# RWKV layer: the projection stage and the start stage get two pools each, the first group's loads move, the last three projections run in quarters

## The chip, the cores and the metric

The kernel runs on one core of one Trainium2 chip. The metric is device time in microseconds, the median of the runs. The engines are TensorE (PE), VectorE (DVE), ScalarE (ACT), GpSimd (POOL) and SyncE (SP, which only issues DMAs here). Each engine, and each engine's DMA queue, runs its instructions in its own order.

## The reference, cut to what matters

The program computes two blocks. The change is in the second one's even layer, an RWKV layer with 12 heads of 64 channels over 256 context and 512 latent tokens:

```python
def proj(h, shift_fn):
    u = h @ w_in
    s, gate_r, four, gate_f = jnp.split(u, [...], axis=-1)
    s = s + (shift_fn(s) - s) * mu                  # r, k0, v, wl, al are neighbour-mixed
    r, k0, v, (wl_f, wl_b), (al_f, al_b) = ...
    return ..., gate_r, four, gate_f

def rwkv_dir_terms(...):                             # for each of two directions
    decay = exp(-exp(-softplus(-(w0 + tanh(wl) @ w2)) - 0.5))
    a = sigmoid(a0 + al @ a2)
    kk = k0 * k_k;  kk = kk / norm(kk per head)
    k = k0 * (1 + (a - 1) * k_a)
    bonus = sum(r * k * r_k per head) * v
    return r, decay, k, v, kk, kk * a, bonus

def step(s, inp):                                    # over the tokens, forward and backward
    sa = einsum('bhij,bhj->bhi', s, kk_t)
    s = s * w_t - sa * b_t + v_t * k_t
    return s, einsum('bhij,bhj->bhi', s, r_t)

def finish(o, gate_r, four, gate_f):
    yr = group_norm(o) * silu(gate_r)
    yf = fourier_mix(four) * silu(gate_f)
    return concatenate([yr, yf]) @ w_out
```

## The kernel before

The even layer has three stages. In the **projection stage** (`even_project`) the input stands channel by channel in on-chip memory, as a high and a low float32r half (`hT`, `cT`). There are 30 projections of 128 output channels; each has eight steps, and a step six matmuls (three products for 512 latent and for 256 context tokens). The weights come through a ring (`weights`: load by SyncE, high half by ScalarE, low half by VectorE). A loop over six pairs of heads j runs, for each direction, low-rank matmuls (`rwkv_lora`), the scaled keys and decays on VectorE (`rwkv_prepare`, tiles `pkr`, `pbk`), and a small triangular product on TensorE (`rwkv_triangle`, tile `sa`), whose diagonal blocks GpSimd inverts later (`rwkv_invert`). Between them stand the projections of pair j + 1 in the order of `ahead_of`: `k0`, `r`, `key`, `v`, where `key` is `rwkv_kk`: a square on ScalarE, head sums on TensorE, a square root, a transpose that spreads it, a product. Then comes the pair's `bonus`, which ends with the tile `po` and its store, and a gate projection for the first four pairs. All results go to DRAM (`sp_kr`, `sp_bk`, `sp_wc`, `sp_v`, `sp_off`, `sp_dia`, `sp_inv`, `sp_o`, `sp_gr`, `sp_four`, `sp_gf`). Left over are projections 24 and 25 (gates of pairs 4 and 5), 26 and 27 (`four`), 28 and 29 (`gf`), and the two triangles of pair 5. Five of these eight pieces (24, triangle, 25, triangle, 26) run while the pool `even_p` is open.

In the **start stage** `rwkv_open` opens the right-hand pool with all tiles of the recurrence; its memory overlaps that of the closed `even_p`, and `reuse_waits="tile"` makes each tile wait for those it overlaps. `rwkv_start` then loads the first chunk group of pairs 0 and 1 (`load`, `load_b`, `load_k`: `wc`, `v`, `bk`, `kr`, ten loads), clears halves of `kr` and `xf`, loads the inverses (`rwkv_inverse`, 14 loads a pair: `xf`, `xt`, `off`), merges the 32-blocks of the inverses to 64 (`rwkv_merges`: `first`, `second`, each for two directions) and makes `values`, `scores`, `keys`. The last three projections (27, 28, 29) stand among them.

In the **chain stage** (`rwkv`) the recurrence runs chunk by chunk (`rwkv_chains`) for two pairs at a time in nine units; each unit's list `fill` of other work (the next group's loads, values, scores and keys) is spread over its slots. TensorE's order there is as written. Before it starts, the pools of `hT`, the weight ring and the first PSUM are closed, and the second group's tiles lie over them.

A scheduler orders the instructions of each engine by their place in the program and by when it expects them to be ready; `high_priority(offset=n)` moves an instruction n places forward, `manual_schedule` keeps TensorE's order as written.

Of the kernel before, what the change touches and what calls it, by code (L numbers as in the profile page):

```python
# [18 lines left out]
P = 128  # L19
# [7 lines left out]
NC = 12  # L27
# [6 lines left out]
HEAD = 0  # L34
HERE = 5
# [18 lines left out]
class Kern:  # L54
# [776 lines left out]
    def even_project(self, pool, hT, cT, sp):  # L831
# [3 lines left out]
        pt = lambda tag, shape, bufs=1, dt=F32: pool.tile(shape, dt, tag=tag, name=self.nm(tag), bufs=bufs)  # L835
# [45 lines left out]
        def gate(pool, n, dst):  # L881

            a, b = dense(n)
            s = pool.tile([P, 768], F32, tag="pg", name=self.nm("pg"), bufs=2)
# [6 lines left out]
        def plain(n, dst, func, pool):  # L891
            a, b = dense(n)
            s = pool.tile([P, 768], F32, tag="pg", name=self.nm("pg"), bufs=2 if pool is self.kp else 1)
# [25 lines left out]
        for j in range(6):  # L919
            q, x = ahead_of(j + 1) if j < 5 else [], terms[j]  # L920
            nc.scalar.dma_start(sp["v"][j], x["v"])
            if j == 5:
                for n in range(26 - LATE, 26 - LATE + EARLY):
                    ahead[n] = self.weights(ins["ev_w_in_2"][n], 1024)
            kds, late = [], []
            for d, (ls, ta) in enumerate(self.rwkv_lora(pt, j, wl, al)):
                kd, *tri = self.rwkv_prepare(pt, j, d, ls, ta, x["r"], x["k0"], x["kk"], sp)
                kds.append(kd)
                late.append(partial(triangles, j, d, *tri))
                if q:  # L930
                    q.pop(0)()
                    late.pop(0)()
            for p in q:
                p()
            self.bonus(pt, j, x["r"], x["v"], kds, sp)
            if j < 6 - LATE:
                gate(pool, 20 + j, sp["gr"][j])

        return ([p for j, f in zip(range(6 - LATE, 6), late)
                 for p in (partial(plain, 20 + j, sp["gr"][j], AF.Silu), partial(lambda f, pool: f(), f))]  # L940
                + [partial(plain, 26 + n, sp["four"][n], AF.Copy) for n in range(2)]
                + [partial(plain, 28 + n, sp["gf"][n], AF.Silu) for n in range(2)])

# [43 lines left out]
    def rwkv_open(self, last):  # L987

        R = self.r = {}
        pool = last.enter_context(self.tc.tile_pool(name="rwkv_l", bufs=1, side="right", reuse_waits="tile"))  # L990
        quads, wide, row = [P, NC, 32], [P, 2, 8, 2, 64], [P, 768]
        for n, shape, ks in (("s0", [P, 2, P], range(4)), ("w", [P, P], range(4)), ("rmask", [P, 256], (0,)),
                             ("sc", [P, 2, 8, P], (0, 2)), ("zs", [P, 8, 2, 64], (0, 2)),
                             ("kr", wide, (0, 2)), ("xf", [P, 2, NC, 64], range(2)), ("bw", [P, 8, P], range(2)),
                             ("wc", [P, 2 * NC], range(4)), ("v", row, range(2)), ("bk", wide, range(2))):
            self.some(pool, n, shape, ks)
        for n in ("xt", "off", "mt"):
            R[n] = pool.tile([P, 4, NC, 32], F32, name=n)
        self.c2["rmask"] = R["rmask"][0]
        self.nc.sync.dma_start(self.c2["rmask"], self.ins["c_rmask"])  # L1000
        self.units, self.sums, self.decay = {}, {}, {}
# [4 lines left out]
    def clear(self, t):  # L1006

        nc = self.nc
        nc.vector.memset(t[64:128, 0], 0.0)
        nc.scalar.activation(t[0:64, 1].rearrange("p i a t -> p i (a t)"), self.ident[0:64, None, :].to_broadcast([64, 8, P]),  # L1010
                             AF.Copy, scale=0.0)

    def clear_xf(self, i):
        for d in range(2):
            for q in (0, 64):
                r = slice(q + 32 * (1 - d), q + 32 * (1 - d) + 32)
                self.nc.scalar.activation(self.r["xf"][i][r, d, :, 32 * d:32 * d + 32],
                                          self.ident[r, None, 0:32].to_broadcast([32, NC, 32]), AF.Copy, scale=0.0)

    def rwkv_start(self, sp, rest):  # L1020

        R = self.r
# [7 lines left out]
        (*inv, load, _), (load_b, load_k, scaled, *work) = zip(*(self.rwkv_begin(j, sp) for j in range(2))), zip(*(self.rwkv_group(j, 0, sp) for j in range(2)))  # L1030
        first = list(zip(load, load_b, load_k, zip(*inv), scaled))
        for l, (v, b, k, i, w) in enumerate(first):
            v()
            b()
            k()
            self.clear(R["kr"][2 * l])
            w()
        for l, (v, b, k, i, w) in enumerate(first):
            for p in i:
# [6 lines left out]
    def rwkv(self, sp, out, mid, last):  # L1046
# [32 lines left out]
        for p in loads(1):  # L1079
            p()  # L1080
# [141 lines left out]
    def rwkv_group(self, j, t, sp):  # L1222
# [9 lines left out]
        kr, bk, sc, zs = R["kr"][i], R["bk"][j % 2][:, (j // 2 + t) % 2], R["sc"][i], R["zs"][i]  # L1232
# [16 lines left out]
        def load_k():  # L1249
            for h in range(2):  # L1250
                nc.sync.dma_start(rows(kr[H[h], h]).rearrange("p (d c) x -> p d (c x)", d=2), sp["kr"][j, H[h], sl])
            self.units[j][t] = kr, sc, zs

        def values():
            v, ps = self.units[j]["v"], self.bank()
# [9 lines left out]
        def keys(k):  # L1265

            ps = self.bank()
# [5 lines left out]
        def scores(d):  # L1273

            pp = [self.bank(), self.bank()]
# [242 lines left out]
    def even_layer(self, hT, dr, held, sp):  # L1518
        tc, nc, ins = self.tc, self.nc, self.ins
        mid, last = ExitStack(), ExitStack()  # L1520
        with (tc.tile_pool(name="subst", bufs=1, reuse_waits="tile") as fp,
# [9 lines left out]
            with tc.tile_pool(name="even_p", bufs=1, reuse_waits="tile") as pool:  # L1531
                self.log_gamma(pool)
                rest = self.even_project(pool, hT, cT, sp)
                for p in rest[:HERE]:
                    p(pool)
            self.rwkv_open(last)
            with tc.tile_pool(name="even_q", bufs=1, reuse_waits="tile") as pool:
                self.rwkv_start(sp, [partial(p, pool) for p in rest[HERE:]])
            self.third = None
        for n in ("h", "w", "ps"):  # L1540
            held[n].close()
        with tc.tile_pool(name="ps_rw", bufs=1, space=PSUM) as self.ps:
            w, rows = self.rwkv(sp, dr["mixed"], mid, last)
# [466 lines left out]
```

## Time and profile before

| | |
|---|---|
| median of 3 runs | 2719.97 us (2709.35 to 2733.05) |
| profiled execution, its own time | 2715.68 us |
| its span | 2713.9 us |
| TensorE busy, mean granted clock | 2543.7 us (94%), 0.976 |
| VectorE, ScalarE, GpSimd busy | 1766.9, 1051.9, 659.5 us |
| projection stage | from about 1640 us |
| first matmul of the chains | 2021.39 us |

All times of rows are microseconds from the start of the profiled execution's span. An idle time in brackets is the engine's wait just before the instruction, with the one that ended it. Line numbers are those of the kernel before.

### The profile page before, as it was taken

How to read it: one execution, taken by the hardware profiler on the slowest of the kernel's cores; microseconds unless marked ns; L12 is line 12 of the kernel's file. 1: busy time of each engine (PE TensorE's matmuls, PEld its weight loads, DVE VectorE, ACT ScalarE, POOL GpSimd, SP SyncE). 2: the span in 40 equal slices, each digit the busy share in tenths (PEclk: the TensorE clock that was granted, in tenths of full speed). 3: DMA queues.
4: the chain of work that ended last, by engine and by line, in shares of the span. 5: the costliest groups of instructions: out<-in, count | busy, mean ns of one | idle time of the engine just before them, and what ended most of it. 6: DMA issues, size and time to landing. Idle time of an engine off the chain costs nothing. (4 is left out here: it accounts for less than half of the span.)

```text
span 2713.9 us, 42105 instructions
## 1 busy us (share of the span) xinstructions
PE 2543.7 (94%) x16408; PEld 2057.5 (76%) x16408; DVE 1766.9 (65%) x3239; ACT 1051.9 (39%) x1859; POOL 659.5 (24%) x735
## 2 busy tenths in 40 slices
PE   7899999999999999999999979999978999899988
PEld 6666788878888666788788868777767887788886
DVE  8878648985348788469975348788538665353263
ACT  3354433344213444424344235444433453332252
POOL 0200111111001101111111020787756342500032
PEclk9999999999999999999999989999979999999999
DMA  4221233543323121225534233456576544022111
GB/s 139 74 67 64 69 117 121 183 150 108 126 78 100 39 84 61 78 95 187 183 125 145 101 130 106 142 163 166 160 197 176 122 128 172 26 76 66 63 47 48
DMA packets 181159, 304.00 MB, mean 112 GB/s; under 512 B 90560, under 2 KB 100416, under 8 KB 180576
## 3 DMA queue, kind: packets, MB, share of 16 engines
q1 hardware_dynamic: 173856, 277.18, 33.0%
q0 software_dynamic: 4224, 15.73, 1.9%
q10 hardware_dynamic: 2880, 8.39, 0.8%
q8 instruction: 130, 2.13, 0.3%
q14 instruction: 69, 0.57, 0.1%
HBM read 255.95 MB, written 45.29 MB: 111 GB/s over the span
## 5 line engine op out<-in xcount | busy, mean ns | idle before, releaser
L108 DVE TENSOR_TENSOR wlo<-raw,whi 128x1024 fp32r<-128x1024 f32 (+1 forms) x335 | 426.5, 1274 | 396.7 <-ACT whi L107 394.4
L120 PE MATMUL psacc<-hT_hi,whi 128*128 128x512 f32 (+1 forms) x1528 | 586.4, 384 | 14.7 <-DVE u L628 7.1
L122 PE MATMUL psacc<-hT_hi,wlo 128*128 128x512 f32 (+1 forms) x1528 | 580.5, 380 | 4.2 <-DVE wlo L108 4.1
L121 PE MATMUL psacc<-hT_lo,whi 128*128 128x512 f32 (+1 forms) x1528 | 582.1, 381 | 2.0 <-POOL hT_lo L115 1.5
L107 ACT ACTIVATE whi<-raw 128x1024 fp32r<-128x1024 f32 (+1 forms) x335 | 323.6, 967 | 632.0 <-PE psacc L121 218.6
L120 PEld LDWEIGHTS psacc<-hT_hi,whi 128*128 128x128 f32 x1528 | 292.2, 191 | 72.4 <-issue 21.2
L122 PEld LDWEIGHTS psacc<-hT_hi,wlo 128*128 128x128 f32 x1528 | 291.7, 191 | 64.1 <-DVE wlo L108 6.8
L121 PEld LDWEIGHTS psacc<-hT_lo,whi 128*128 128x128 f32 x1528 | 292.3, 191 | 52.6 <-issue 8.5
L167 POOL TENSOR_TENSOR rr<-rr,mhalf 128x1 f32<-128x1 f32 (+1 forms) x52 | 49.8, 962 | 495.0 <-DVE rr L162 495.0
L637 POOL TENSOR_TENSOR gl<-silu,gh 128x512 fp32r<-128x512 f32 x44 | 66.0, 1500 | 406.9 <-ACT gh L636 406.9
L1300 POOL TENSOR_TENSOR fs_m<-fs_g,fs_x 112x31 f32<-112x31 f32 (+15 forms) x186 | 134.5, 723 | 40.5 <-DMA fs_g<-sp_dia 26.4
L1302 POOL TENSOR_TENSOR fs_x<-fs_x,fs_m 112x31 f32<-112x31 f32 (+15 forms) x186 | 133.5, 718 | 14.6
L683 DVE CUSTOM_DVE_ANT_0 psmm<-adaw,adac 128x512 f32<-128x512 f32 x192 | 132.3, 720 | 6.6 <-ACT adac L677 6.6
L156 PE MATMUL psacc<-whi,ohT_lo 128*128 128x512 f32 x256 | 100.2, 392 | 0.8 <-POOL ohT_lo L115 0.8
L154 PE MATMUL psacc<-whi,ohT_hi 128*128 128x512 f32 x256 | 100.5, 393 | 0.0
L155 PE MATMUL psacc<-wlo,ohT_hi 128*128 128x512 f32 x256 | 100.1, 391 | 0.0
L376 PE MATMUL psacc<-wlo,gh 128*128 128x512 f32 x246 | 96.8, 394 | 0.0
L377 PE MATMUL psacc<-whi,gl 128*128 128x512 f32 x246 | 96.8, 394 | 0.0
L375 PE MATMUL psacc<-whi,gh 128*128 128x512 f32 x246 | 96.8, 393 | 0.0
L342 POOL TENSOR_TENSOR m<-m,gate 128x512 f32<-128x512 f32 x16 | 20.6, 1286 | 303.6 <-DVE gate L341 303.6
L476 DVE SCALAR_TENSOR_TENSOR cvy<-cvu,lconst,cvy 128x512 f32<-128x512 f32 x120 | 89.3, 766 | 1.4
L516 PE MATMUL psmm<-kT,qq 64*128 64x256 f32 (+3 forms) x224 | 72.2, 549 | 15.8 <-DVE smx L591 13.6
(590 smaller groups left out, 5337.3 us busy)
## 6 DMA issues: line engine op xcount, KB each, us to landing
raw<-w_up SPq DMA_DIRECT2D x88, 512.0 KB, 3.3
raw<-w_fm SPq DMA_DIRECT2D x60, 512.0 KB, 3.3
adaw<-ada_w SPq DMA_DIRECT2D x96, 256.0 KB, 2.8
raw<-w_down SPq DMA_DIRECT2D x44, 512.0 KB, 3.3
raw<-ev_w_in SPq DMA_DIRECT2D x30, 512.0 KB, 4.0
raw<-od_w_tm SPq DMA_DIRECT2D x24, 512.0 KB, 3.3
sp_kr<-pkr SPq DMA_DIRECT2D x12, 768.0 KB, 3.5
bk<-sp_bk SPq DMA_DIRECT2D x18, 512.0 KB, 6.3
```

Source lines behind the costliest of these rows:

```text
L107: nc.scalar.activation(hi[:, :n], raw[:, :n], AF.Copy)
L108: (eng or nc.vector).tensor_tensor(lo[:, :n], raw[:, :n], hi[:, :n].bitcast(F32), ALU.subtract)
L120: mm(out, whi, xhi, start=start, stop=False)
L121: mm(out, whi, xlo, start=False, stop=False)
L122: mm(out, wlo, xhi, start=False, stop=stop)
L154: mm(o[:, :ncol], xhi[:, k, sl], wh, start=k == 0, stop=False)
L155: mm(o[:, :ncol], xhi[:, k, sl], wl, start=False, stop=False)
L156: mm(o[:, :ncol], xlo[:, k, sl], wh, start=False, stop=k == nk - 1)
L375: mm(acc, xh[k][:, ts], w[0][:, s], start=k == 0, stop=False)
L683: nc.vector.tensor_tensor_reduce(d, w, c[:, j, :], 1.0, 0.0, ALU.mult, ALU.add, part[:, half, n, j:j + 1])
L1300: nc.gpsimd.tensor_tensor(mv, g[:, :t, t:t + 1].to_broadcast([112, t, w]), x[:, t:t + 1, t:].to_broadcast([112, t, w]), ALU.mult)
L1302: nc.gpsimd.tensor_tensor(x[:, :t, t:], x[:, :t, t:], mv, ALU.subtract)
```

## The change

The projection stage's pool is split in two: `even_l` (outer) holds `pkr`, `pbk`, `sa`, `pg`; `even_p` (inner) holds the rest and closes earlier. The recurrence's pool is split too: `rwkv_l` holds what the first loads fill and what the merges read, and is opened as soon as `even_p` closes; `rwkv_m` holds the rest and is opened after the triangles. The order at the end of the projection stage becomes: projection 24, bonus 5, loads of the first group and of the inverses (`rwkv_load`), projection 25, triangle, projection 26, triangle. In `ahead_of`, `v` goes ahead of `key`. The clears all run on VectorE. The last three projections are cut into quarters of two steps and stand with the merges, values, scores and keys in one written order for TensorE; the stores of 28 and 29 are issued by SyncE in `rwkv`, behind the second group's loads. Cut to its core (left out: the constants `HEAD` and `HERE`, the lines that only pass arguments on, `clear_xf`, which gets memsets like `clear`, and `slot` in `rwkv_group`):

```diff
-        pt = lambda tag, shape, bufs=1, dt=F32: pool.tile(shape, dt, tag=tag, ...)
+        pt = lambda tag, shape, bufs=1, dt=F32: (later if tag in ("pkr", "pbk", "sa") else pool).tile(
+            shape, dt, tag=tag, name=self.nm(tag), bufs=bufs)
...
+        def in_parts(n, dst, func, buf):
+            st = {}
+            def part(i):
+                if not i:
+                    st["w"] = self.weights(ins["ev_w_in_2"][n], 1024)
+                    st["ps"] = self.acc(), self.psum("av", 1) if n % 2 else self.acc()
+                (hi, lo), (a, b) = st["w"], st["ps"]
+                for k in (2 * i, 2 * i + 1):
+                    ks = slice(k * P, (k + 1) * P)
+                    for o, (xhi, xlo) in ((a, hT), (b[:, :256], cT)):
+                        self.mm3(o, hi[:, ks], lo[:, ks], xhi[:, k], xlo[:, k], k == 0, k == KT - 1)
+                if i == 3:
+                    s = buf()
+                    with self.tc.high_priority(offset=DRAIN):
+                        nc.scalar.activation(s[:, lat], a, func)
+                        nc.scalar.activation(s[:, ctx], b[:, :256], func)
+                    st["out"] = s
+            return [partial(part, i) for i in range(4)], lambda: (nc.scalar if n == 27 else nc.sync).dma_start(dst, st["out"])
...
-            return [partial(project, j, "k0", 6), partial(project, j, "r", 0), partial(key, j), partial(project, j, "v", 12)]
+            return [partial(project, j, "k0", 6), partial(project, j, "r", 0), partial(project, j, "v", 12), partial(key, j)]
...
-            self.bonus(pt, j, x["r"], x["v"], kds, sp)
+            if j < 5:
+                self.bonus(pt, j, x["r"], x["v"], kds, sp)
...
+        return (partial(plain, 24, sp["gr"][4], AF.Silu), lambda: self.bonus(pt, 5, x["r"], x["v"], kds, sp),
+                [partial(plain, 25, sp["gr"][5], AF.Silu), late[0], partial(plain, 26, sp["four"][0], AF.Copy), late[1]],
+                lambda bufs: [in_parts(n, dst, f, b) for (n, dst, f), b in
+                              zip(((27, sp["four"][1], AF.Copy), (28, sp["gf"][0], AF.Silu), (29, sp["gf"][1], AF.Silu)), bufs)])
...
     def clear(self, t):
-        nc.vector.memset(t[64:128, 0], 0.0)
-        nc.scalar.activation(t[0:64, 1].rearrange(...), self.ident[0:64, None, :].to_broadcast([64, 8, P]), AF.Copy, scale=0.0)
+        for h in range(2):
+            nc.vector.memset(t[64 - 64 * h:128 - 64 * h, h], 0.0)
...
+        begun, groups = ([f(j) for j in range(2)] for f in (lambda j: self.rwkv_begin(j, sp), lambda j: self.rwkv_group(j, 0, sp)))
+        for (*_, load, _), (load_b, load_k, *_) in zip(begun, groups):
+            load()
+            load_b()
+            load_k()
+        for inv0, inv1, *_ in begun:
+            inv0()
+            inv1()
+        self.first = [g[2:] for g in groups]
+
+    def rwkv_start(self, sp, rest):
+        for l, (w, *_) in enumerate(self.first):
+            self.clear_xf(l)
             w()
+            self.clear(self.r["kr"][2 * l])
+        a, b = (q[1:] for q in self.first)
+        first, second = ([p for j in range(2) for p in self.rwkv_merges(j)[i:i + 2]] for i in (0, 2))
+        (store, *stores), (x, y, z) = [r[1] for r in rest], [r[0] for r in rest]
+        with self.tc.manual_schedule(engines={mybir.EngineType.PE}):
+            for p in (x[:1] + first[:2] + x[1:2] + first[2:] + x[2:3] + second[:2] + x[3:] + [store] + second[2:] + a[:2] + y[:1] + a[2:4]
+                      + y[1:2] + a[4:] + y[2:3] + b[:2] + y[3:] + b[2:4] + z[:1] + b[4:] + z[1:]):
                 p()
-            self.clear_xf(l)
-        work = [q[0] for q in work] + mixed(self.rwkv_merges(0) + self.rwkv_merges(1), [q[1] for q in work])
-        for p in rest[:HEAD] + mixed(rest[HEAD:], work):
-            p()
+        return stores
...
-        for p in loads(1):
+        for p in loads(1) + stores:
             p()
...
-            with tc.tile_pool(name="even_p", bufs=1, reuse_waits="tile") as pool:
-                self.log_gamma(pool)
-                rest = self.even_project(pool, hT, cT, sp)
-                for p in rest[:HERE]:
-                    p(pool)
-            self.rwkv_open(last)
+            with tc.tile_pool(name="even_l", bufs=1, reuse_waits="tile") as later:
+                with tc.tile_pool(name="even_p", bufs=1, reuse_waits="tile") as pool:
+                    self.log_gamma(pool)
+                    gate, bonus, rest, tiles = self.even_project(pool, later, hT, cT, sp)
+                    gate()
+                    bonus()
+                self.rwkv_open(last)
+                self.rwkv_load(sp)
+                for p in rest:
+                    p()
+            self.rwkv_more(last)
             with tc.tile_pool(name="even_q", bufs=1, reuse_waits="tile") as pool:
-                self.rwkv_start(sp, [partial(p, pool) for p in rest[HERE:]])
-            self.third = None
+                self.third = None
+                own = lambda: pool.tile([P, 768], F32, tag="pg", name=self.nm("pg"), bufs=1)
+                other = lambda: hp.tile([P, 1024], F32, tag="raw", name=self.nm("raw"), bufs=1)[:, :768]
+                stores = self.rwkv_start(sp, tiles((own, other, own)))
```

## Rows read from the trace of the kernel before

**Rows 1.** Stretches: us, engines' busy time (instructions), TensorE clock, DMA share, GB/s.

```profile
1920.00:1940.00 20.00, 13.88 (x74) 10.79 (x72) 19.96 (x16) 8.73 (x14) 18.82 (x16) 1.00 0.59 186
1940.00:1960.00 20.00, 19.35 (x179) 17.08 (x180) 7.54 (x7) 8.03 (x15) 17.89 (x28) 0.91 0.54 151
...
2000.00:2020.00 20.00, 14.70 (x320) 13.15 (x318) 6.50 (x14) 8.11 (x16) 17.27 (x33) 0.57 0.69 179
2020.00:2040.00 20.00, 16.00 (x292) 13.86 (x286) 13.00 (x33) 7.08 (x22) 8.79 (x17) 0.75 0.69 177
```

**Rows 2.** TensorE's timeline, 1926 to 2030: start, us, instruction [idle before, released by].

```profile
1929.43 1.53 PE L1442 MATMUL psmm<-bsum,c_blk 128*128 128x512 f32 x4 [3.48 <-DVE bsum L1439]
...
1940.65 2.29 PE L1196 MATMUL psmm<-pkr,pbk 64*64 64x64 f32 x48 [3.28 <-DVE po L1443]
...
2004.77 2.07 PE L1278 MATMUL pstr<-kr,bk 64*128 64x128 f32 x8 [4.32 <-ACT mt L1338]
...
2021.39 0.69 PE L1386 MATMUL psch<-zs,kr 64*64 64x64 f32 x7 [1.17 <-ACT xf L1349]
...
2028.88 1.38 PE L1278 MATMUL psms<-kr,bk 64*128 64x128 f32 x10
```

**Rows 3.** SyncE's queue in order of time, 1940 to 2010.

```profile
1943.34 0.92 SPq L1444 DMA_DIRECT2D sp_o<-po  x1
...
1962.92 0.38 SPq L1211 DMA_DIRECT2D wc<-sp_wc  x1
...
1970.18 2.84 SPq L1251 DMA_DIRECT2D kr<-sp_kr  x2
...
2002.10 1.33 SPq L1314 DMA_DIRECT2D xf<-sp_inv  x3
...
2008.04 0.47 SPq L1319 DMA_DIRECT2D off<-sp_off  x1
```

**Rows 4.** Waits of SyncE's queue, 1960 to 2010: total us, times, longest.

```profile
SPq L1314 <- DMA sp_gf<-pg: 11.8, 2, 9.1
...
SPq L1314 <- DMA kr<-sp_kr: 3.4, 1, 3.4
```

**Rows 5.** Timelines of ScalarE and VectorE, 1984 to 1999.

```profile
1984.54 0.60 ACT L894 ACTIVATE pg<-psacc 128x512 f32<-128x512 f32 x1 [8.35 <-DMA sp_four<-pg]
...
1996.67 0.60 ACT L894 ACTIVATE pg<-psacc 128x512 f32<-128x512 f32 x1 [7.81 <-PE psacc L122]
...
1997.15 0.91 DVE L1009 MEMSET kr<- 64x1024 f32 x1 [6.09 <-PE psacc L122]
```

**Rows 6.** TensorE's waits in the loop, 1645 to 1925: total us, times, longest.

```profile
PE psmm L1112 <- ACT sa L1197: 12.3, 4, 5.8
```

**Rows 7.** TensorE's timeline, first and sixth step of projection 26.

```profile
1946.74 0.50 PE L120 MATMUL psacc<-hT_hi,whi 128*128 128x512 f32 x1
...
1952.08 0.40 PE L120 MATMUL psacc<-hT_hi,whi 128*128 128x512 f32 x1
```

**Rows 8.** VectorE's timeline, pair 2 (1753 to 1770) and pair 5 (1930 to 1945).

```profile
1760.05 0.96 DVE L1172 TENSOR_TENSOR kd<-kd,pj 128x768 f32<-128x768 f32 x1 [5.35 <-ACT kd L1166]
1760.93 2.76 DVE L878 SCALAR_TENSOR_TENSOR pj<-psacc,e_mus,pj 128x504 f32<-128x504 f32 x5
...
1939.92 1.01 DVE L1443 TENSOR_TENSOR po<-psmm,pj 128x512 f32<-128x512 f32 x2
```

**Rows 9.** DMA issues, 1962 to 2015: KB each, median us to landing.

```profile
kr<-sp_kr SPq DMA_DIRECT2D x8, 256.0 KB, 8.2
...
xf<-sp_inv SPq DMA_DIRECT2D x16, 48.0 KB, 2.5
```

**Rows 10.** Chain that ended last, 2030 to 2080: start, us, piece, instructions.

```profile
2032.29 1.14 PE psms L1278 x16
...
2070.09 1.02 PE psms L1269 x8
...
2072.99 1.64 PE psms L1334 x96
```

More of the change, by code (lines that the diff above doesn't have):

```diff
@@ L829, in consts2, with even_project @@
         nc.vector.tensor_scalar(e["c1"], e["c2"], -1.0, 1.0, ALU.mult, ALU.add)
-    def even_project(self, pool, hT, cT, sp):
+    def even_project(self, pool, later, hT, cT, sp):
         nc, ins, e = self.nc, self.ins, self.e
-        pt = lambda tag, shape, bufs=1, dt=F32: pool.tile(shape, dt, tag=tag, name=self.nm(tag), bufs=bufs)
+        pt = lambda tag, shape, bufs=1, dt=F32: (later if tag in ("pkr", "pbk", "sa") else pool).tile(
+            shape, dt, tag=tag, name=self.nm(tag), bufs=bufs)
         R = self.r = {}
@@ L879, in shifted, with gate @@
             return s
-        def gate(pool, n, dst):
+        def gate(n, dst):
             a, b = dense(n)
-            s = pool.tile([P, 768], F32, tag="pg", name=self.nm("pg"), bufs=2)
+            s = later.tile([P, 768], F32, tag="pg", name=self.nm("pg"), bufs=2)
             with self.tc.high_priority(offset=DRAIN):
@@ L889, in gate, with plain @@
             nc.scalar.dma_start(dst, s)
-        def plain(n, dst, func, pool):
+        def plain(n, dst, func):
             a, b = dense(n)
-            s = pool.tile([P, 768], F32, tag="pg", name=self.nm("pg"), bufs=2 if pool is self.kp else 1)
+            s = later.tile([P, 768], F32, tag="pg", name=self.nm("pg"), bufs=2)
             nc.scalar.activation(s[:, lat], a, func)
@@ L934, in even_project @@
                 p()
-            self.bonus(pt, j, x["r"], x["v"], kds, sp)
+            if j < 5:
+                self.bonus(pt, j, x["r"], x["v"], kds, sp)
             if j < 6 - LATE:
[L937 to L942, printed above, removed]
+                gate(20 + j, sp["gr"][j])
+        return (partial(plain, 24, sp["gr"][4], AF.Silu), lambda: self.bonus(pt, 5, x["r"], x["v"], kds, sp),
+                [partial(plain, 25, sp["gr"][5], AF.Silu), late[0], partial(plain, 26, sp["four"][0], AF.Copy), late[1]],
+                lambda bufs: [in_parts(n, dst, f, b) for (n, dst, f), b in
+                              zip(((27, sp["four"][1], AF.Copy), (28, sp["gf"][0], AF.Silu), (29, sp["gf"][1], AF.Silu)), bufs)])
     def fourier(self, sp, out):
@@ L1029, in rwkv_start, with rwkv @@
         self.bank = bank
[L1030 to L1036, printed above, removed]
-            w()
-        for l, (v, b, k, i, w) in enumerate(first):
-            for p in i:
-                p()
-            self.clear_xf(l)
-        work = [q[0] for q in work] + mixed(self.rwkv_merges(0) + self.rwkv_merges(1), [q[1] for q in work])
-        for p in rest[:HEAD] + mixed(rest[HEAD:], work):
-            p()
-    def rwkv(self, sp, out, mid, last):
+        begun, groups = ([f(j) for j in range(2)] for f in (lambda j: self.rwkv_begin(j, sp), lambda j: self.rwkv_group(j, 0, sp)))
[10 more added lines that the diff above has]
+            self.clear_xf(l)
+            w()
+            self.clear(self.r["kr"][2 * l])
[5 more added lines that the diff above has]
+                      + y[1:2] + a[4:] + y[2:3] + b[:2] + y[3:] + b[2:4] + z[:1] + b[4:] + z[1:]):
+                p()
+        return stores
+    def rwkv(self, sp, out, mid, last, stores):
         nc, ins = self.nc, self.ins
@@ L1265, in keys @@
         def keys(k):
-            ps = self.bank()
+            ps, sc = self.bank(), R["sc"][slot]
             for i in range(4):
@@ L1542, in even_layer @@
         with tc.tile_pool(name="ps_rw", bufs=1, space=PSUM) as self.ps:
-            w, rows = self.rwkv(sp, dr["mixed"], mid, last)
+            w, rows = self.rwkv(sp, dr["mixed"], mid, last, stores)
         return mid, w, rows
```

37 lines of the change are left out of this document (18 added, 19 removed).

## The prediction

> **What bounds the kernel now.** I read the page's busy table first: TensorE is busy for 94% of the span, VectorE for 65%, and the chain that ended last runs mostly over matmuls. So only stretches where TensorE waits or runs at its lower clock can give time back. The table of stretches by 20 us shows one [rows 1]: from 1940 to 2020 us TensorE falls from 19.35 to 14.70 us busy and the granted clock from 0.91 to 0.57, while VectorE and ScalarE are two thirds idle (6.50 and 8.11 us in the last of them). No engine bounds this stretch, waits do. Here the last projections end and the first merges, scores and keys are made, before the chains of the recurrence begin at 2021.4 us [rows 2]. The reader is to see two kinds of wait. On TensorE's timeline [rows 2]: 3.48 and 3.28 us ahead of the last bonus and the first triangle of head pair 5, and 4.32 us ahead of the second pair's scores. On SyncE's queue [rows 3]: the group's loads begin at 1962.92 us, behind the triangles' stores, and the loads of the inverses go on until 2008.5 us, because two of them wait 11.8 us for the stores `sp_gf` of the last projections [rows 4]. Such a store is issued only when its projection is done, so loads of inverses wait for projections on TensorE, and merges wait for these loads. ScalarE repeats this: its drain of `gf[0]` waits 8.35 us for the store before it, since there is one `pg` buffer [rows 5].
>
> A second place is the loop over the head pairs: TensorE waits 12.3 us in four pieces before the head sums of `rwkv_kk` [rows 6].
>
> **The change part by part.** All terms are against the profiled execution: 2715.68 us, span 2713.9; the median of the three runs is 2719.97, some 4 us more. A measurement of this kernel tells about 1% (27 us) from no change.
>
> *Term 1, `v` in front of `key`.* The projection of `v` now runs where TensorE waited for the square of `kk`. Five steps of a projection take 5.34 us [rows 7], 1.07 us each, so its eight take 8.5 us. The stall of 12.3 us is what can be won. But the head sums then start later: by 8.5 us less the stall of that turn, 8.5 - 12.3 / 4 = 5.4 us on average. Behind them stand the square root, the spread, `kk`, the matmuls of `al` (which take their banks after the spread) and `kd`, with which VectorE's long block begins; VectorE waits 5.35 us for the last part of this chain [rows 8] and is then full to the triangles. What pays it back: `v`'s shift (2.76 us [rows 8] and a sixth instruction like these five, 0.55) and the drain of the bonus (1.01 us) leave that block for the idle piece ahead of it, 4.3 us a turn. So a turn loses about 1 us where VectorE sets the pace and wins the whole stall where TensorE does. Ends: -12.3 us and +4 us. VectorE is busy for 19.96 of 20 us in the block's last turn [rows 1], which keeps me from the lower end. I take -5.
>
> *Term 2, bonus and triangles of pair 5.* The bonus now follows the gate's projection, the triangles follow projections 25 and 26. The two stalls (3.48 + 3.28 us) are VectorE's backlog, which ends at 1940.9 us with `po` [rows 8]; the work that would fill them, the weights' low halves for projection 26, stands in the same backlog. Ends -6.8 and 0; I take -4, since term 1 takes `v`'s shift out of this backlog too.
>
> *Term 3, the start stage.* Removed: the loads' place behind the triangles' 12 stores, the coupling of the inverses' loads to the last stores (two of those now come last), ScalarE's clears, the wait of the one `pg` buffer (the three projections have two places). Added: the loads need the memory of the pool that closes, which `po` may free last; its store is issued at 1943.34 us and takes 0.92 us of the queue [rows 3], so the loads begin near 1944 on before's clock. The group's ten loads took 10.1 us to issue (1962.92 to 1973.02), the inverses' then waited 3.4 us on a landing [rows 4], and the last 13 of them, which waited for nothing, took 6.4 us (2002.10 to 2008.51, [rows 3]), 0.49 us each. So 1944 + 10.1 + 3.4 = 1957.5; 14 issues for pair 0 end at 1964.4, and with a landing of 2.5 us [rows 9] they are there at 1966.9; pair 1's at 1973.8.
> TensorE, in the order now written out: projection 26 begins at 1946.7 behind the last triangle [rows 7] and ends at 1955.2, a quarter of 27 (2.1 us) at 1957.3. Then it waits for pair 0's inverses, 9.6 us; two first merges of 0.82 us (96 matmuls took 1.64 us, [rows 10]) and a quarter bring 1970.6; it waits 3.2 us for pair 1's; two merges, 1975.4. What is left waits for nothing that I find: two quarters 4.2, four second merges 3.3, projections 28 and 29 17.0, four `scores` of 1.14, four `keys` of 0.51 (a row holds two) and two `values`, four transposes each like `keys` [rows 10]: 4.6 + 2.0 + 1.0. Together 32.1, to 2007.5. The two waits bring half-clock matmuls behind them and the interleaved drains some gaps: 2 us. The chains then begin at 2009.5 instead of 2021.4: -12. The clears move to VectorE, which has 13 us free in 2000 to 2020 [rows 1], and cost nothing here. Ends: -25 if the inverses come before TensorE asks (the two waits, 12.8 us, go too), +6 if the loads again stand behind the triangles' stores (17.8 us later, to 1961.8). I take -12. Of the last three stores, projection 27's is issued by ScalarE behind its drain, the others by SyncE behind the next group's loads; only the Fourier part, far later, reads them.
>
> *Term 4, what the earlier start runs into.* The second group's `kr` tiles lie where the weight stream's buffers were, and projection 29 holds one of these to its end. Before, it ended at 1996.7 us (its drain, [rows 5]), 24.7 us ahead of the chains; now it is the last thing ahead of them. The `kr` loads can start some 2 us behind it (four issues of 0.5 us stand before them) and land in 8.2 us [rows 9], 10.2 us into the chains, while the first chain asks for them with its first scores 7.5 us in (2028.88, [rows 2]). TensorE's order is fixed there, so it waits 2.7 us. The clears for that group fall there too: four of 0.91 us [rows 5] and eight of 384 columns instead of 1024, 0.34 us each by that row, 6.4 us on VectorE, which has 7 us free in 2020 to 2040 [rows 1]; 0.3 us. Together +3. Ends: 0, and +9 where the clears stand ahead of the chains' own work.
> The Trainium skill, page DMA: Bandwidth & Descriptors, section Anatomy of one DMA, gives 2.0 us plus bytes / 436e3 for one transfer on the GpSimd path. For the 256 KB of a `kr` load this makes an estimate of 2.6 us where the row of SyncE's queue says 8.2. By the page the second group's loads would be in time, this term would be 0.3, and the total some 3 us lower.
>
> Sum: -5 - 4 - 12 + 3 = -18, so 2715.7 - 18 = **2698 us**.
>
> **The rivals.**
> *The cover holds* (faster by over 1%): the inverses land before TensorE needs them, because most of the closed pool is read for the last time before `po`, and TensorE sets the pace of the loop. Then term 1 is near -9, term 2 near -6, term 3 near -22, term 4 +3: -34, 2682 us. For it: the waits of [rows 2] and [rows 6] and the clock of 0.57 are worth more than that. Against it: SyncE issues in order, so one tile that comes late holds every load behind it.
> *The waits only change place* (no change): terms 1 and 2 near zero because VectorE's backlog ends no earlier, term 3 near -7, term 4 +3: 2712 us. For it: VectorE's 19.96 of 20 us [rows 1].
> *The fixed order holds the work up* (slower): the first merges stand second in the order, and 32 us of projections, scores and keys stand behind them, which before ran while the inverses were late. The order wins only while pair 1's inverses land before 1983 us on before's clock (2021.4 less 32.1, 1.6, 2 and term 4's 3), or 1992 with terms 1 and 2. Behind the triangles' stores (1961.8) they would land at 1991.6; one further wait like the 9.1 us piece of [rows 4] makes it 2000.7, and the kernel 9 us slower, 2725 us. For it: the triangles' stores become ready at about the moment when the closed pool does. Against: in program order the loads stand first.
>
> **How the numbers follow.** Forecast (2688 to 2708) 0.44, the cover holds 0.31, the waits change place 0.16, the fixed order holds up 0.09. The range reaches from inside the first rival, 2674, to inside the last, 2722. Faster by over 1%: the first rival and the lower edge of the forecast, 0.36; slower by over 1%: 0.07, as its price is mostly below 1%; within 1%: 0.57.
>
> **What would show it.** Term 1: the head sums no longer wait on TensorE; right if new waits at the triangles or at the banks of `al` stay under 8 us over the loop. Term 2: the two gaps of some 3 us ahead of the last triangles gone. Term 3: the group's first `wc` load some 16 us nearer to the last `po` store; TensorE waiting about 10 and 3 us at the first merges; no load of `xf` waiting on `sp_gf`; a clock above 0.8 in the stage. Term 4: a wait of 2 to 9 us ahead of the first scores inside the chains, released by `kr`. The prediction is wrong if the loads start long before `po`'s store, if SyncE lets the triangles' stores pass, or if a weight load of projections 26 to 29 is caught behind loads that wait for memory, which would show as TensorE waiting for `wlo`.

## The result, and the profile after

The change made the kernel slower: 2751.84 us (median of 4 runs, 2747.16 to 2760.74) against 2720.15 us (4 runs of the kernel before beside them), ratio 1.0122, 95% interval 1.01 to 1.0144. The forecast was 2698 us. The profiled execution took 2751.42 us, its span 2749.7 us: 35.8 us more than the span before. Both timelines have the same landmarks, so the 35.8 us can be cut at them: TensorE's first wait for `cT_hi`, early in the projection stage and ahead of the loop (the *mark*; L118 after, L120 before), the end of the last `po` (L1480 after, L1443 before, on VectorE), the first matmul of the chains (L1423, L1386), and the additions to `o` that close each of the nine chains (L1468, L1431).

| stretch | before, us | after, us | difference |
|---|---|---|---|
| start of the span to the mark | 1622.1 | 1622.4 | +0.3 |
| mark to the last `po` (the loop) | 318.8 | 329.5 | +10.7 |
| last `po` to the first chain (start stage) | 80.5 | 80.3 | -0.2 |
| first chain | 27.4 | 35.8 | +8.4 |
| chains 2 to 9 (third +4.0, sixth +5.3) | 215.8 | 226.9 | +11.1 |
| behind the chains | 449.3 | 454.8 | +5.5 |

**The loop lost instead of winning.** TensorE's waits in the kernel after, 1645 to 1955 us (total, times, longest), answer to [rows 6]:

```profile
PE psmm L1233 <- DVE pbk L1210: 15.7, 3, 12.2
PE psacc L120 <- DVE wlo L106: 7.7, 1, 7.7
...
PE psmm L1149 <- ACT sa L1234: 0.3, 1, 0.3
```

The 12.3 us before the head sums are gone, down to 0.3. In their place TensorE waits 15.7 us before triangles, for `pbk`, and 7.7 us, ahead of the last bonus, for the low half of projection 26's weights, which VectorE makes behind its block. One piece of the 15.7 is 12.24 us, on TensorE's timeline of pair 2 (the last row is ScalarE's drain of `v` of this pair):

```profile
1745.31 1.28 PE L1176 MATMUL pstr<-al,a 64*128 64x256 f32 x4
1758.82 2.82 PE L1233 MATMUL psmm<-pkr,pbk 64*64 64x64 f32 x48 [12.24 <-DVE pbk L1210]
1763.87 2.15 PE L1233 MATMUL psmm<-pbk,pkr 64*64 64x64 f32 x34 [2.23 <-DVE pbk L1210]
...
1776.09 0.69 ACT L872 ACTIVATE pj<-psacc,e_om 128x512 f32<-128x512 f32 x1 [6.32 <-PE psacc L120]
```

The low-rank matmuls of `al` end at 1746.6 us and nothing stands between them and the triangles. The scheduler did not put `v` of pair 2 ahead of its head sums, as the line asks: it stands behind the triangles, with the gate projection of pair 1 and the next pair's `k0` and `r`. In the kernel before `v` (drained at 1759.91 us), this gate and this `k0` ran between the head sums at 1744.15 us and the triangles at 1782.00. VectorE prepares both directions in one block meanwhile, as the stretch shows (columns as in [rows 1]): it is busy for 18.78 of 20 us, TensorE for 7.25.

```profile
1740.00:1760.00 20.00, 7.25 (x45) 4.25 (x46) 18.78 (x20) 11.60 (x19) 18.75 (x17) 0.77 0.49 151
```

**The start stage gained nothing.** SyncE's queue answers to [rows 3]:

```profile
1955.78 0.46 SPq L1248 DMA_DIRECT2D wc<-sp_wc  x1
...
1965.64 0.33 SPq L1249 DMA_DIRECT2D v<-sp_v  x1
...
1987.35 0.47 SPq L1356 DMA_DIRECT2D off<-sp_off  x1
...
1994.97 1.57 SPq L104 DMA_DIRECT2D raw<-ev_w_in  x2
...
2033.87 3.64 SPq L1288 DMA_DIRECT2D kr<-sp_kr  x4
```

The loads begin 3.9 us behind `po` (forecast: 3.1). But the second pair's `v` is held up, the weights of projections 28 and 29 (`raw`) come only when all loads of inverses and the triangles' last stores are issued, and the second groups' `kr` comes at 2033.87 us, when the first chain already runs. The queue's own waits, 1950 to 2095 us, answer to [rows 4]:

```profile
SPq L1490 <- DMA sp_inv<-fs_g: 20.4, 1, 20.4
...
SPq L1249 <- DMA sp_four<-pg: 6.3, 1, 6.3
```

TensorE's timeline, 1970 to 2050 us, answers to [rows 2]:

```profile
1977.54 0.28 PE L1371 MATMUL psmm<-xt,off 32*32 32x32 f32 x2 [13.98 <-DMA off<-sp_off]
1984.52 1.40 PE L1371 MATMUL psmm<-xt,off 32*32 32x32 f32 x45 [6.70 <-DMA off<-sp_off]
...
2044.07 2.90 PE L1315 MATMUL psms<-kr,bk 64*128 64x128 f32 x16 [7.52 <-DMA kr<-sp_kr]
```

Both waits of 13.98 and 6.70 us are in pair 0's first merge (most of it needs a second `off`, which lands 7 us after the first). The last row is the wait inside the first chain, which began at 2032.23 us.

### The profile page after: what moved, and what is told of

The parts are those of the page before. It is cut to its first block, busy times and chain, and to the rows that moved or that the text cites. A ratio compares the mean times of both kernels' runs of the same rounds, so it can differ in the third digit from the quotient of the medians.

```text
span 2749.7 us, 42127 instructions
## 1 busy us (share of the span) xinstructions
PE 2544.3 (93%) x16408; PEld 2059.5 (75%) x16408; DVE 1780.5 (65%) x3259; ACT 1041.7 (38%) x1839; POOL 660.5 (24%) x735
## 3 DMA queue, kind: packets, MB, share of 16 engines
q1 hardware_dynamic: 174144, 277.96, 33.3%
## 5 line engine op out<-in xcount | busy, mean ns | idle before, releaser
L118 PE MATMUL psacc<-hT_hi,whi 128*128 128x512 f32 (+1 forms) x1528 | 586.5, 384 | 14.9 <-DVE u L626 7.2
L120 PE MATMUL psacc<-hT_hi,wlo 128*128 128x512 f32 (+1 forms) x1528 | 578.5, 379 | 11.3 <-DVE wlo L106 11.3
L118 PEld LDWEIGHTS psacc<-hT_hi,whi 128*128 128x128 f32 x1528 | 291.7, 191 | 74.1 <-issue 21.7
L120 PEld LDWEIGHTS psacc<-hT_hi,wlo 128*128 128x128 f32 x1528 | 290.9, 190 | 71.0 <-DVE wlo L106 13.6
L635 POOL TENSOR_TENSOR gl<-silu,gh 128x512 fp32r<-128x512 f32 x44 | 66.1, 1503 | 407.3 <-ACT gh L634 407.3
L514 PE MATMUL psmm<-kT,qq 64*128 64x256 f32 (+3 forms) x224 | 72.0, 550 | 15.7 <-DVE smx L589 13.4
```

The lines of the kernel that those rows point to most:

```text
L118: mm(out, whi, xhi, start=start, stop=False)
L120: mm(out, wlo, xhi, start=False, stop=stop)
```

## The experiments

Expectations speak of theories: A, that values ahead of the key step lengthen the loop; B, that projection 29 keeps the memory of the second groups' tiles to the end; C, that SyncE's store does; D, that TensorE lacks the weights of projections 28 and 29 while it waits for inverses; E, that the load of `gr` holds up SyncE; F, that a late store of ScalarE does. Ratios are to the kernel before, run beside each kernel on the same chip, so they compare better than the medians do.

**The order of `v` and `key`.** Two kernels: the change with the line put back, and the kernel before with the line alone.

```diff
-return [..., partial(project, j, "r", 0), partial(project, j, "v", 12), partial(key, j)]
+return [..., partial(project, j, "r", 0), partial(key, j), partial(project, j, "v", 12)]
```

> The changed kernel with one line put back: in the loop over head pairs the key step stands ahead of the values again. Theory A (values ahead of the key step is what lengthened the loop): the last bonus ends near 1941 instead of 1952, TensorE's 15.7 us of waiting for pbk at the triangles fall under 5, its wait for head sums comes back at 8 to 12, and the time falls by 8 to 13 us, to 2739 to 2744. Rival (the pool split did it: pkr, pbk and sa now live in a pool of their own and wait for other buffers): the last bonus stays within 3 us of 1952 and the time within 4 us of 2752.

Measured: 2740.51 us, ratio 1.0072 (1.0053 to 1.0091), against 1.0122 of the change: 11 us by the medians, 14 by the ratios. The last `po` ended at 1937.2 us, 318.6 us behind the mark (before: 318.8, the change: 329.5), and TensorE's waits have the old form again (same view as above):

```profile
PE psmm L1149 <- ACT sa L1234: 12.3, 4, 5.8
...
PE psmm L1233 <- DVE pbk L1210: 1.3, 2, 0.8
```

The seven later variants of the change with `key` first, w28_ahead apart, ended `po` between 1931.9 and 1939.9 us; the change and its two variants with `v` first between 1950.4 and 1951.9. Theory A holds, and the split of the pools costs the loop nothing that shows.

> The kernel before with that one line changed alone (values ahead of the key step). Theory A: the last bonus ends 8 to 13 us later than 1941 and the kernel takes 2728 to 2734 us. Rival (pool split, or the forecast's own term): no longer than the kernel before, 2713 to 2722 us, with the head-sums wait of 12.3 us gone.

Measured: 2723.62 us, 1.0016 (0.9996 to 1.0035), `po` at 1945.3 us, only 4.4 us later than before. But this execution was already ahead at the mark, where the line has no part yet. The mark of the kernel before, that of this kernel, and this kernel's pair 2:

```profile
1622.11 0.38 PE L120 MATMUL psacc<-cT_hi,whi 128*128 128x256 f32 x1 [2.94 <-DMA cT_hi<-dr_cT]
1615.95 0.38 PE L120 MATMUL psacc<-cT_hi,whi 128*128 128x256 f32 x1 [3.12 <-DMA cT_hi<-dr_cT]
...
1752.14 2.82 PE L1196 MATMUL psmm<-pkr,pbk 64*64 64x64 f32 x48 [12.24 <-DVE pbk L1173]
```

From the mark to `po` it took 329.4 us, 10.5 us more than before, with the same wait of 12.24 us: the line costs the loop as much here as in the changed kernel, and theory A holds in both. Over all kernels traced the mark lies between 1615.95 and 1625.31 us, so a `po` by the clock of the span can mislead by some us. In time the loss is 4 us with an interval that reaches 1; what gave the rest back was not settled (the start stage was 3.0 us shorter).

**Projection 29 ahead of the second pair's pieces.**

```diff
-  + y[1:2] + a[4:] + y[2:3] + b[:2] + y[3:] + b[2:4] + z[:1] + b[4:] + z[1:]
+  + y[1:] + a[4:] + z + b
```

> The changed kernel with its fixed TensorE order altered: projections 28 and 29 whole ahead of the second pair's values, scores and keys, instead of projection 29 ending right before the chains. Theory B (the second groups' clears and loads wait until projection 29 lets go of its inputs' memory, so they fall into the first chain): clears and kr loads of the second groups begin 7 to 10 us ahead of the chains, the 7.5 us wait for kr inside the first chain falls under 2, the first chain takes 26 to 28 us instead of 34.4, and the time falls by 6 to 11 us, to 2741 to 2746. Rival (SyncE's queue and the DMA engines are the limit, the loads land late in any case): the kr wait stays over 5 us, or the chains begin later by what the waits shrink; within 4 us of 2752.

Measured: 2752.02 us, 1.0112 (1.0081 to 1.0142), no gain, though the first chain fell from 35.8 to 28.2 us as theory B says. The third rose from 34.1 to 49.1. TensorE's row and SyncE's wait:

```profile
2113.57 0.76 PE L1315 MATMUL psms<-kr,bk 64*128 64x128 f32 x2 [21.93 <-DMA kr<-sp_kr]
```

```profile
SPq L1490 <- DMA sp_inv<-fs_g: 34.8, 1, 34.8
```

L1490 is the load of `gr` for the norm of the first two pairs. It waits for the last inversion on GpSimd, and everything behind it on SyncE waits too, the third groups' `kr` first. That is theory E; the change shows the same wait with 20.4 us.

**ScalarE's stores.** One edit: the stores of projections 28 and 29 go back to ScalarE's queue.

> The changed kernel with the stores of projections 28 and 29 issued by ScalarE as before the change, not by SyncE ahead of the second groups' o and kr loads. Theory C (SyncE's queue is blocked by the store that waits for projection 29's drain): kr loads begin earlier by 5 us or more and the time falls by 5 to 8 us. Theory B (the memory is let go only when projection 29 ends, so the clears, which wait for TensorE, come no earlier than 2031): kr loads begin at most 2 us earlier, time within 3 us of 2752.

Measured: 2749.66 us, 1.0101 (1.006 to 1.0142), no difference from the change that can be told; the second groups' `kr` loads at 2033.3 us instead of 2033.9. Theory C falls, B holds.

**What keeps the start stage at 80 us.** Four kernels on top of key_first. In the first, the weights of projections 25 to 28 are asked for ahead of the first groups' loads (`ahead.update(...)` before `rwkv_load`), and the list becomes `x + [store] + y[:2] + first[:2] + y[2:] + first[2:] + second + a[:2] + z[:2] + a[2:] + z[2:] + b`.

> The kernel of the run key_first (2740.5 us) with the weight loads of projections 25 to 28 issued ahead of the first groups' loads, and TensorE's list altered so that projections 27 and 28 fill the wait for the first merges: 27 whole, half of 28, first merges of pair 0, the rest of 28, first merges of pair 1, second merges, then 29 between the first pair's scores and keys. Theory D (the start stage gains nothing because TensorE stands before the first merges, 20 us in all, while projections 28 and 29, whose weights are queued on SyncE behind 36 loads of inverses, are still to be done): the waits at the first merges fall under 8 us, the chains begin 10 to 16 us earlier after the last bonus than the 84.0 of key_first, and the time falls to 2724 to 2731 us. Rival (the stage is bound by its transfers: the same bytes and packets in another order): the weights only push the inverses' loads back by as much, chains begin within 4 us of 84, time within 5 us of 2740.

Measured: 2748.42 us, 1.0111 (1.009 to 1.0132), 11 us slower than key_first by the ratios, with intervals that just touch. The start stage did shrink, from 84.0 to 76.6 us, and the waits for `off` to 12.3 us. But `po` ended 11 us later: 6.8 of these lie ahead of the mark, where the edit does nothing, and 4.4 in the loop, where two low halves of weights (3.3 us) now stood ahead of it on VectorE. And SyncE stood 32.1 us at `gr`, which made the third chain 48.0 us instead of 33.3.

> The kernel of key_first with the first groups' loads put behind the last gate, the triangles and projection 26 again in program order (the split of the pools and TensorE's fixed order stay). Theory D: the loads in front are worth nothing, since they hold up the triangles' stores and the weights; without them the time stays within 5 us of 2740. Rival (the forecast's: early loads are what shortens the start): chains begin 8 to 20 us later, time 2748 to 2760 us.

Measured: 2742.6 us, 1.0086 (1.006 to 1.0112): no difference from key_first that can be told; the start stage 87.1 us against 84.0. But `po` came 3.2 us sooner behind the mark, and from the mark the chains begin after 402.5 us against 402.6: the early loads, the heart of the change, are worth nothing there that shows.

> The kernel of key_first without the fixed TensorE order in the start stage: the same pieces, in quarters, left to the scheduler. Theory D: an order made ready by ready does not wait 14.8 us at one merge, and projection 29 ends earlier, so the kr wait in the first chain goes: chains begin 3 to 10 us earlier, time 2728 to 2738 us. Rival (the order is not the limit): within 4 us of 2740.

Measured: 2738.52 us, 1.0071 (1.0043 to 1.0099), start stage 83.7 us. The fixed order neither costs nor brings anything that can be told.

> The kernel of key_first with projection 29 ahead of the second pair's values, scores and keys, and with the load of gr for the first two pairs moved from SyncE's queue to GpSimd's, behind the inversions that it waits for in any case. Theory E (what p29_early gained in the first chain it lost in the third, because SyncE stood 34.8 us at the gr load, whose memory is let go by the last inversion, with the third groups' kr loads behind it): the first chain falls from 32.6 to about 28, the third from 33.3 to 28 to 30, no kr wait over 2 us is left, time 2728 to 2734 us. Rival (the third chain's loads wait for the chain before and the DMA engines, not for gr): the third chain stays over 32 us, time over 2735 us.

Its second edit is `(nc.gpsimd if j < 2 else nc.sync).dma_start(state["g"], sp["gr"][j])`. Measured: 2736.98 us, 1.0071 (1.0052 to 1.009). The first chain took 27.9 us and the third 25.1, and no wait for `kr` is left, as theory E says. In time it is a draw with key_first by the ratios, though the profiled execution was 7.8 us shorter. The start stage took 88.4 us instead of 84.0, but only because `po` came sooner (from the mark the chains begin after 402.9 us against 402.6); the fourth chain took 32.6 instead of 28.5.

> The kernel before the change with one edit: gr of the first two pairs is loaded through GpSimd's queue, behind the inversions, instead of SyncE's. Theory E says that SyncE's 10.3 us at that load, ahead of the third groups' loads, costs the kernel before too: its third chain falls from 30.1 to 25 to 28 and the time by 2 to 6 us, to 2713 to 2717 us. Rival (only the changed kernel, whose inversions end later, is hurt): within 2 us of 2718.65.

Measured: 2721.5 us, 1.0024 (1.0013 to 1.0034), a little slower, third chain 31.5 us. Theory E is no use to the kernel before, where this wait was 10.3 us against 20.4 in the change.

**The store that holds the loads.** The program gives each transfer of SyncE and ScalarE the next of eight semaphores in turn, and a transfer waits until the one that had its semaphore before has landed. From the changed kernel's list for SyncE:

```
sp_off<-sa   waits semaphore 3, ScalarE
sp_dia<-sa   waits semaphore 5
...
v1<-sp_v     waits semaphore 4
```

Semaphore 4 went to ScalarE's store of projection 26 (`sp_four`), issued at 1960.78 us; the second pair's `v` needs nothing else. Moving that store behind the loads on SyncE (`(nc.sync if n == 26 else nc.scalar).dma_start(dst, s)`) takes the wait away.

> The kernel of p29_gr (2737.0 us) with the store of projection 26 moved from ScalarE's queue to SyncE's, where it stands behind the loads of inverses. Theory F (the transfers of SyncE and ScalarE take turns on eight semaphores, so that a load waits until the transfer eight places ahead has landed, and the late store of projection 26 holds the second pair's kr load and the 36 loads of inverses behind it for 7.0 us): that wait goes, the loads of off land 5 to 7 us earlier, the 25 us of TensorE's waits at the first merges fall to 18 to 20, the chains begin 4 to 7 us earlier and the time falls to 2730 to 2733 us. Rival (the transfers themselves are the limit): the wait moves to the next load and the time stays within 3 us of 2737.

Measured: 2728.39 us, 1.0055 (1.0038 to 1.0072). The wait is gone, TensorE's waits at the first merges fell from 25.0 to 18.7 us, the start stage from 88.4 to 84.9. So the wait is what theory F says, but its price is not shown: pair 0's inverses came 32.7 us behind `po` instead of 33.8, not 5 to 7 us earlier (pair 1's merges are what no longer waits), the chains begin 404.1 us behind the mark against 402.9, and by the ratios the gain is 4 us, with intervals that overlap.

> The kernel before with the stores of projections 26 to 29 issued by GpSimd instead of ScalarE, so that SyncE's loads of inverses, which waited 11.8 us for the stores to sp_gf and 11.6 us for those to sp_four, no longer do. Theory F applied to the kernel before: these waits go, the chains begin 3 to 8 us earlier after the last bonus than 80.5, time 2708 to 2714 us. Rival (those waits are hidden, or GpSimd's inversions are held up by the stores): within 3 us of 2717, or slower.

Measured: 2775.27 us, 1.0218 (1.0196 to 1.024). GpSimd issued the first of these stores at 2020.95 us, behind an inversion; ScalarE's next drain needed the one `pg` buffer and waited 64.0 us for it, and TensorE stood 60.4 us behind that. So this says nothing about theory F in the kernel before, only that a store must not be put behind long work on its queue.

**Weights or list.** Fed is four_sync with the list of w28_ahead and the early weights, their split now behind the last bonus; list_alone has the list without the weights.

> The kernel of four_sync with the weights of projection 28 fetched ahead of the first groups' loads (their split on ScalarE and VectorE behind the last bonus, so that it does not hold the loop up as in w28_ahead) and the TensorE list of w28_ahead. Theory D: the last bonus stays within 3 us of four_sync, chains begin 70 to 76 us after it instead of some 82, the third chain is not held by gr, and the time is 2718 to 2727 us, level with the kernel before or a little behind. Rival (transfers are the limit): chains begin 80 us or more after the last bonus, time over 2730 us.

> The kernel of four_sync (2728.4 us) with the TensorE list of fed, without the early fetch of projection 28's weights. Theory D (the weights are what lacked): TensorE now stands before projection 28 instead of before the merges, until weights that are queued behind the inverses' loads are there; chains begin 83 us or more after the last bonus, time 2728 to 2738 us. Rival (the list alone does it): 76 to 79 us after the last bonus, time 2719 to 2724 us.

Measured: fed 2720.92 us, 1.0022 (1.0008 to 1.0036), start stage 75.5 us; list_alone 2742.7 us, 1.01 (1.0075 to 1.0126), start stage 88.4. TensorE's waits of both, 1930 to 2080 us, list_alone first:

```profile
PE psacc L118 <- ACT whi L105: 29.0, 1, 29.0
```

```profile
PE psmm L1372 <- DMA off<-sp_off: 9.0, 3, 5.9
```

With the same order of work, TensorE waits 29.0 us for projection 28's weights in the one and 9.0 for `off` in the other: the weights' loads are issued at 1984.1 us behind the inverses in list_alone, ahead of the loads in fed. The chains begin 15.0 us sooner behind the mark in fed (392.3 against 407.3), and 7.0 sooner than in the kernel before. Theory D holds. The rival of the transfers falls for the weights; for the inverses it is not excluded, since TensorE still waits for `off`.

**The clears.** In fed the first chain still takes 31.2 us. Fed_clear shares the clears with ScalarE again, as the kernel before did.

> The kernel of fed (2720.9 us) with the clears of kr and xf shared with ScalarE again, as before the change. Term 4 of the forecast (clears on VectorE in the first chain: 3 us, bounds 0 and 9): in fed the four of kr and the eight of xf stand between 2012.8 and 2021.6 ahead of the copy of zs that TensorE waits for, so the first chain falls from 31.2 to 27 to 28 and the time by 2 to 5 us, to 2716 to 2719 us, level with the kernel before. Rival (ScalarE's clears stand ahead of its own zs and w copies and cost as much there): within 1.5 us of 2721.

Measured: 2720.47 us, 1.0015 (0.9998 to 1.0032), first chain 29.2 us. Two us of the chain, nothing in time that can be told. This is the best version of the change: 29 us faster than it by the ratios, level with the kernel before, not ahead of it.

**Measured from the mark.** `po` itself moves with VectorE's order, so the start stage alone can mislead; the sum shows when the chains begin.

| kernel | mark to `po`, us | start stage | sum |
|---|---|---|---|
| before | 318.8 | 80.5 | 399.3 |
| the change | 329.5 | 80.3 | 409.8 |
| key_first | 318.6 | 84.0 | 402.6 |
| loads_behind | 315.4 | 87.1 | 402.5 |
| p29_gr | 314.6 | 88.4 | 402.9 |
| four_sync | 319.2 | 84.9 | 404.1 |
| list_alone | 318.9 | 88.4 | 407.3 |
| fed | 316.9 | 75.5 | 392.3 |
| fed_clear | 319.4 | 73.5 | 392.8 |

So fed's chains begin 7.0 us sooner than before, and what it wins there it loses behind: 3.8 us in the first chain, 5.8 in the sixth and 5.6 behind the chains.

## Why the prediction was wrong, step by step

*Term 1* (forecast -5, ends -12.3 and +4) is the step that failed most: +11 us in the loop, outside its ends (the line alone: 10.5 in the kernel before, 10.9 between key_first and the change). The stall of 12.3 us went, as it said. What failed is the premise that the line moves `v` alone: I weighed the delay of the head sums against VectorE's idle piece, turn by turn, and never asked what TensorE has left to do while VectorE prepares both directions. In the turns of pairs 1, 4 and 5 `v` did go ahead of the head sums, and no wait for `pbk` above 1.3 us came of it: other projections still stood beside the block. In pair 2's turn the scheduler put `v`, the gate and the next `k0` behind the triangles, and TensorE, which keeps that order, waited 12.24 and 2.23 us. Why the scheduler did so was not tried.

*Term 2* (-4, ends -6.8 and 0): nothing that shows. `po` of key_first ended 3.7 us earlier than before, but its first head sums, at 1650.48 us, were already 3.8 us ahead of before's 1654.23; its two gaps are still 3.7 and 2.0 us. In the change they are gone, and the 7.7 us for projection 26's low half stand there instead: VectorE's backlog stayed. Before_v_first has that wait too (7.4 us), so it comes with term 1's line.

*Term 3* (-12, ends -25 and +6): -0.2. The loads began about where the step put them. Pair 0's inverses were forecast 26.0 us behind `po` (1966.9 - 1940.9) and came 32.6 behind it (1984.52 - 1951.9). The 6.6 us are a sum of larger errors: the ten loads took 12.2 us, SyncE's wait of 6.3 us for `sp_four` among them, instead of 13.5; the fourteen issues for pair 0 took 10.2 instead of 6.9; and from the last of them to TensorE 6.4 us passed instead of 2.5, while the DMA engines were full (a share of 1.08 to 1.29 from 1978 to 1984 us). Taking the wait away brought such inverses only 1.1 us nearer to `po` (four_sync against p29_gr). In [rows 4] I read the same sort of wait as a load that waits for projections and thought it removed with the last two stores; it was a place in the turn of semaphores, and projection 26's store took the next one. "What is left waits for nothing that I find" failed too: the weights of 28 and 29 stood behind the inverses' loads, ScalarE waited 10.79 us for them at 1999.16 us, with the merges' drains behind it. This is the part that has a cure: with the weights ahead of the loads, and projection 27 and half of 28 ahead of the first merges, the chains begin 11.8 us sooner behind the mark (fed against four_sync). From the end of pair 0's first merges, 1987.2 us, to the chains it took 45.0 us; the forecast had 41.0 for the same pieces and the wait for pair 1, which did not come. So 7.7 us late at these merges and 4.0 behind them: -12 became -0.3. The text named a weight load caught behind other loads as what would make it wrong, but gave it no place in the sum.

*Term 4* (+3, ends 0 and +9): +8.4, the right mechanism, mis-sized. The `kr` loads began at 2033.87 us, 2.3 us behind projection 29, against 2 forecast, and landed in 10.1 us (median) instead of 8.2. The first chain asked for them at 2036.5, 4.3 us in and not 7.5, and behind 7.52 us of waiting its clock was 0.50 until 2050. The clears, 0.3 in the sum, cost 2 us of this chain in fed (31.2 against 29.2 in fed_clear). In this row the estimate by the Trainium skill's figure for the GpSimd path, 2.6 us for such a load (DMA: Bandwidth & Descriptors, Anatomy of one DMA), lies further off than in [rows 9]: the 10.1 us of the row decide.

*Not in the sum:* 11.1 us in the later chains and 5.5 us behind them. Of the third chain p29_early and p29_gr show the cause, SyncE standing at `gr`. The rest was not settled: the variants of the change took 453 to 457 us behind the chains, against 449.3 before, and the sixth chain took 24.4 us before and 28 to 31 in all but fed_clear (25.7) and p29_early (24.6). Before_v_first has 28.4 us there too, so the longer sixth chain is not the changed pools' alone.

The rival *the fixed order holds the work up* gave the right sign and the wrong reason: no_fixed shows no cost of the order. Against the forecast of -18 the sum is off by 53.8 us: 20.0 up to the last `po`, 11.8 in the start stage, 5.4 in the first chain, 16.6 not foreseen.

## What to carry to other kernels

Before a stall is filled by moving work into it, ask what each engine has left to do in every turn afterwards, and where a scheduler sets the order, read the new order from the trace: here one moved line left one turn of six with nothing for TensorE beside VectorE's block, which was longer than the stall. Loads put in front of a stage are in front of everything that shares their queue, so go through the queue and its semaphores for what now comes behind them; the weights of the work meant to hide the loads go first. And where a wait is cured, look at once which later transfer stands next in that queue: three edits here only moved the wait (first chain to third, head sums to triangles, inverses to weights). And compare stages from a landmark ahead of the edit: two readings of `po` alone would have been off by more than 6 us.

## What the runs showed of the hardware

TensorE stopped in the middle of groups of like matmuls, with no releaser. Two stops of the changed kernel, on TensorE's timeline in the third chain:

```profile
2095.35 0.88 PE L1383 MATMUL psms<-xf,mt 32*32 32x32 f32 x44
2099.74 0.32 PE L1383 MATMUL psms<-xf,mt 32*32 32x32 f32 x4 [3.51 <-issue]
...
2104.08 2.95 PE L1315 MATMUL psms<-kr,bk 64*128 64x128 f32 x16 [2.97 <-issue]
```

One packet of kind instruction (0.02 MB) was moved in 2097 to 2098 us, inside the first stop, while the other transfers took the DMA engines whole (share 1.00, 383 GB/s from 2092 to 2098). The granted clock was 0.50 from 2100 to 2108 us, that is 1.2 GHz, so the work behind the stops was slowed as well. The Trainium skill (Runtime: NRT & Kernel Launch, Instruction fetch mechanics) says that code is streamed in blocks of 16 KiB over a queue of its own and that the cost of a block's end is mostly hidden; whether these stops are such ends was not tried. The sixth chain has one of 2.45 us that ends at 2182.51 us, with an instruction packet only behind it in 2183 to 2185 us and no other transfer in 2181 to 2183, so full DMA engines are not its cause. Such stops are not the change's alone: before_gr has one of 2.39 us at 2022.10 us.
